# Longer times for GpSimd's operations in a scheduler's table: the same instructions of a two-layer encoder in another order

## The chip, the core and the metric

The kernel runs on one core of one Trainium2 chip. The metric is the device time of one execution in microseconds (us), the median of several runs. An engine is named as in the profile: PE is TensorE (matrix products and transposes), PEld its loading of the stationary operand, DVE is VectorE, ACT is ScalarE, POOL is GpSimd, and SP is SyncE, which here only issues DMAs.

## The reference

Two layers, each a mixer and a gated FFN, over 256 tokens of 1024 channels, in float32. Cut to what matters:

```python
def mixer_sublayer(x, n1, w_in_l, qg, kg, rpb_l, og, w_out_l, tables):
    h = rms_norm(x, n1)
    qa, ka, va, qd, kd, vd, qc, kc, vc = split(h @ w_in_l)
    out_a = neighbourhood_attention(norm(qa), norm(ka), va, rpb_l)      # 4 heads, position bias
    out_d = dilated_window_attention(rotary(norm(qd)), rotary(norm(kd)), vd)   # 6 heads, 3 window patterns
    out_c = gqa_block_attention(axial(norm(qc)), axial(norm(kc)), vc)   # 6 heads on 2 key heads
    mix = concat([rms_norm(out_a), rms_norm(out_d), rms_norm(out_c)])
    return x + mix @ w_out_l

def channel_sublayer(x, n2, w_gu, cw, cb, w_dn):
    g, u = split(rms_norm(x, n2) @ w_gu)           # 2 x 2816
    g = depthwise_conv_centred(g, cw, cb)          # 3 taps along the sequence
    return x + (gelu(g) * u) @ w_dn

for l in range(2):
    x = mixer_sublayer(x, ...)
    x = channel_sublayer(x, ...)
```

Every head has 64 channels. The norm of a head is a root mean square over these 64, so each token and head needs a power of −1/2.

## The kernel before, in words

**The numbers.** To keep float32 accuracy each operand of a large product is split into a high and a low part, and each product is three matmuls: high by high, high by low, low by high (`mm3`). ACT makes the high part of a weight (`wp_hi`) from what was loaded (`wp_raw`), DVE the low part (`wp_lo`), in chunks of 512 elements. The same is done for the activations (`act_hT`, the normed input turned; `act_mixT_hi` and `act_mixT_lo`, the heads' outputs; `act_ch` and `act_cl`, the turned probabilities).

**The mixer.** A weight comes in units of at most 2048 elements per partition, each loaded by one DMA of SP. The seven projections are, in this order, the queries, keys and values of the dilated heads ("d"), the queries and then keys with values of the grouped-query heads ("c"), and the queries with keys, then the values of the neighbourhood heads ("a"). Each goes to two accumulators in PSUM (two blocks of 128 tokens), from a pool of four slots, `psa`. `normed` then squares the accumulator (ACT), sums per head, computes the mean square (`small_ms`, one instruction on POOL) and its power of −1/2 (`small_rstd`, one on POOL, by `rstd_of`), and scales the accumulator by it (DVE, `act_z`); this reading sets the slot free for a later projection. Dilated and grouped-query heads are then rotated (DVE, `act_sw` and `act_z`, with tables that POOL makes in `tables_d` and `tables_c`), and all are turned by PE. Heads go two by two: twelve score matmuls as one burst that nothing may interrupt, a maximum (`small_nm`, or for heads with a bias an addition with minimum, `act_s2k` of the custom DVE instruction), the exponential on ACT, the reciprocal of the sum, the turning of the probabilities by PE, and the product with the values. The output of two heads is split into `act_mixT`; its square is added up (`act_sqm`, one addition on POOL per pair of heads after the first). The output projections of the three groups go to `psa` again, and DVE adds each to the residual `const_x`, scaled by the group's own power (`group_rstd`, POOL again).

**The position bias** of the neighbourhood heads is made in layer 0 on the way: POOL repeats a small table (`na_repeat`, the copy `act_nab<-act_few`), SP writes it to a scratch in DRAM and reads it back along diagonals (`na_diagonals`), and DVE adds the mask in three instructions (`na_bias_mask`).

**The FFN** has eleven steps of 256 channels. A step holds gate and up (64 matmuls), the convolution and gelu on ACT and DVE, and the product down of an earlier step (24 matmuls).

**What sets the order.** No instruction is issued where the code calls it. All of them are recorded in a `Plan` with their dependences (`add`), then `order` simulates the five engines: it repeatedly takes, over all engines, the instruction that could start soonest, and among those that tie the one of the lower rank, which is the place in the code plus a shift. An instruction's length comes from `cost`; from engine to engine a delay is added from the table `HANDOVER`; DMAs wait for the wires; buffers of a pool come in the order of the code, and an instruction that first uses a buffer waits for a slot. At the end `emit` calls them all in this order, so every instruction in the profile has line 402. The order of each engine is then fixed: on the chip an engine waits at an instruction whose inputs aren't ready, with all that is behind it.

In the model's table an instruction of POOL costs, in ns for n elements per partition: memset 40 + 0.9 n; copy 3.4 n; power 300 + 165 n; anything else 2.2 n + 160. The functions that the change and the steps touch are `cost` (line 405, the edit at 439 to 441), `order` (298, where `o.ns` is used), `rstd_of` (600), `mean_squares` (632), `tables_d` and `tables_c` (733, 748), `mixed` (1017) and `na_repeat` (715). A power has n = 6 for the dilated heads and the grouped-query queries, 2 for the grouped-query keys, 8 for the neighbourhood queries with keys, and 2 (two blocks of tokens) for a whole row or a group.

Of the kernel before, what the change touches and what calls it, by code (L numbers as in the profile page):

```python
# [216 lines left out]
class Plan:  # L217
# [30 lines left out]
    def add(self, engine, method, args, kw):  # L248
# [14 lines left out]
        if method == "matmul" and not kw["start"]:  # L263
            ins.append(args[0])
        o.ns, o.size = cost(engine.name, method, args, kw, ins)
        o.before, o.after, o.first, o.tiles = set(), [], [], []
        for v in ins + outs:
# [137 lines left out]
def cost(engine, method, args, kw, ins):  # L405

    out = args[0]
    if method == "dma_start":
        w = out if isinstance(out, View) else args[1]
        small = min(out.shape[-1], args[1].shape[-1]) < 128  # L410
        return 460, 4 * math.prod(w.shape) * (2 if small else 1)
    n = out.width()
    psum = any(v.tile.pool.psum for v in ins)
    if engine == "PE":
        if method == "transpose":
            return 110, 0
        n = args[2].width()
        if args[1].dtype == F32:
            return 108, 0
        if args[1].shape[0] < P:  # L420
            return n / 4.8 + 15, 0
        return n / (2.4 if args[1].dtype == F32R else 1.2) + 2.5, 0
    if engine == "ACT":
        extra = 93 * sum(isinstance(kw.get(k), View) for k in ("scale", "bias")) + 90 * ("accum_out" in kw)
        return 0.833 * n + (47 if psum else 94) + extra, 0
    if engine == "DVE":
        if method in ("reduce_sum", "reduce_max"):
            n = args[1].width()
        per = 1.04
        if method in ("tensor_copy", "tensor_scalar_mul") and not psum:  # L430
            per = 0.52
        if method == "tensor_tensor_reduce":
            per = 1.3
        return per * n + (130 if method == "scalar_tensor_tensor" or method == "tensor_scalar_mul" and n > 16 else 70), 0
    if method == "memset":
        return 40 + 0.9 * n, 0
    if method == "tensor_copy":
        return 3.4 * n, 0
    if kw.get("op") == ALU.pow:
        return 300 + 165 * n, 0  # L440
    return 2.2 * n + 160, 0


@with_exitstack
# [959 lines left out]
```

## Time and profile before

| | us |
|---|---|
| runs | 618.57, 619.05, 619.42 |
| median | 619.05 |
| the profiled execution | 618.73 |
| its span, from first to last instruction in the trace | 616.9 |
| PE busy | 607.5 |
| DVE busy | 487.1 |
| ACT busy | 429.8 |
| POOL busy, in 125 instructions | 78.1 |
| layer 0: second half of the FFN's first gate matmuls begins | 129.39 |
| layer 1: the same | 430.96 |

How to read it: the profiled execution lies 0.32 us under the median, and 1.83 us of it lie outside the span. In the views below a row gives the start and the length in us, the engine, the line, the operation, the output, an arrow and the inputs, the shapes and the count. In brackets stands how long the engine was idle just before and whose work ended it. A buffer is named by its pool and tag, so all accumulators of `psa` are `psa_a`, and those of the second PSUM pool, for scores, transposes, heads' outputs and gate and up, are `psw_w`. PE's matmuls are pipelined: the length of one contains its way through, so the distance from start to start tells the rate. The mixer of a layer runs about 130 us, the rest is the FFN. In both layers the FFN's first gate matmuls are in two halves, by the two halves of the channels of its normed input, which is turned by eight transposes each, and the second half needs the last output projections to be in the residual.

POOL's work is spread thinly: it is busy 3.55 us of the 20 from 60 to 80, and 5.89 of the 20 from 80 to 100. TensorE's granted clock was 1.00 in both.

### The profile page before, as it was taken

The numbers are of one execution on the slowest core, as the hardware profiler recorded it, in microseconds if no ns is written. First come the engines' busy times: TensorE is split into PE (matmuls) and PEld (weight loads), VectorE is DVE, ScalarE is ACT, GpSimd is POOL, SyncE is SP. The second block draws the span as 40 slices with busy tenths as digits, with TensorE's granted clock in tenths as the row PEclk, the third lists the DMA queues.
The fourth block names the chain that finished last, engine by engine and source line by source line (L and its number), as shares of the span: only waits on it lengthen the run. The fifth ranks groups of instructions, "written<-read, shape, count | busy, mean of one in ns | idle before, by whom it ended". The sixth has DMA issues, their size and how long they took to land.

```text
span 616.9 us, 9838 instructions
## 1 busy us (share of the span) xinstructions
PE 607.5 (98%) x3496; PEld 525.4 (85%) x3496; DVE 487.1 (79%) x1000; ACT 429.8 (70%) x1064; POOL 78.1 (13%) x125
## 2 busy tenths in 40 slices
PE   8999999999999999999999999999999999999997
PEld 6998888878888888888899989887888888888885
DVE  4898888897878777777867798979877777787775
ACT  6888898777565565556588899897756566556651
POOL 2732130111600000000023212112000000000000
PEclk9999999999999999999999999999999999999999
DMA  8894303466596566554444632127575565556501
GB/s 276 270 285 163 104 34 105 143 218 198 195 225 224 176 201 204 198 169 162 154 147 151 232 104 86 35 73 247 181 236 172 188 206 192 166 189 203 178 29 68
DMA packets 81345, 104.66 MB, mean 170 GB/s; under 512 B 9464, under 2 KB 68952, under 8 KB 81296
## 3 DMA queue, kind: packets, MB, share of 16 engines
q1 hardware_dynamic: 80720, 103.51, 52.0%
q8 instruction: 27, 0.44, 0.3%
q10 hardware_dynamic: 576, 0.53, 0.3%
q14 instruction: 22, 0.18, 0.1%
HBM read 102.54 MB, written 1.49 MB: 169 GB/s over the span
## 4 chain that ended last, share of the span: by engine, by line
PE 93%; ACT 3%; DVE 2%; DMA 1%; issue 1%; ACTq 0%
PE psw_w L402 49%; PE psa_a L402 44%; ACT act_s2k L402 2%; DMA const_x<-in_x_dram 1%; DVE wp_lo L402 1%; DVE act_hT L402 1%; ACT act_ch L402 0%; DVE const_x L402 0%; ACTq L402 0%; ACT wp_hi L402 0%; DVE small_nm L402 0%; ACT act_mixT_hi L402 0%; DVE act_z L402 0%; ACT act_sqm L402 0%; DVE small_rs L402 0%
## 5 line engine op out<-in xcount | busy, mean ns | idle before, releaser
L402 DVE TENSOR_TENSOR wp_lo<-wp_raw,wp_hi 128x512 fp32r<-128x512 f32 (+2 forms) x348 | 244.5, 732 | 48.2 <-ACT wp_hi L402 46.3
L402 PE MATMUL psw_w<-act_hT,wp_hi 128*128 128x512 f32 x704 | 247.8, 397 | 2.7 <-DVE act_hT L402 2.7
L402 ACT CAST wp_hi<-wp_raw 128x512 fp32r<-128x512 f32 (+2 forms) x348 | 213.0, 659 | 25.0 <-PE psw_w L402 15.7
L402 PE MATMUL psw_w<-act_hT,wp_lo 128*128 128x256 f32 x704 | 195.8, 279 | 0.0
L402 PEld LDWEIGHTS psw_w<-act_hT,wp_hi 128*128 128x128 f32 x704 | 131.9, 188 | 35.1 <-DVE act_hT L402 3.9
L402 PEld LDWEIGHTS psw_w<-act_hT,wp_lo 128*128 128x128 f32 x704 | 132.6, 188 | 1.1
L402 PE MATMUL psa_a<-wp_hi,act_hT 128*128 128x384 f32 (+2 forms) x448 | 113.4, 333 | 0.0
L402 ACT COPY act_s2k<-psw_w 128x256 f32<-128x256 f32 x88 | 32.4, 373 | 80.5 <-PE psw_w L402 80.5
L402 PEld LDWEIGHTS psa_a<-wp_hi,act_hT 128*128 128x128 f32 x448 | 78.7, 190 | 2.4
L402 PE MATMUL psa_a<-wp_lo,act_hT 128*128 128x384 f32 (+2 forms) x224 | 75.0, 335 | 0.0
L402 PE MATMUL psa_a<-wp_lo,act_ch 128*128 128x512 f32 x176 | 69.5, 395 | 0.0
L402 PE MATMUL psa_a<-wp_hi,act_ch 128*128 128x512 f32 x176 | 69.3, 394 | 0.0
L402 PE MATMUL psa_a<-wp_hi,act_cl 128*128 128x512 f32 x176 | 66.1, 394 | 0.0
L402 DVE TENSOR_TENSOR act_s2k<-psw_w,act_s2k 128x256 f32<-128x256 f32 x88 | 36.8, 422 | 30.6 <-ACT act_s2k L402 30.2
L402 PEld LDWEIGHTS psa_a<-wp_lo,act_hT 128*128 128x128 f32 x224 | 42.4, 189 | 2.0 <-DVE wp_lo L402 1.1
L402 PEld LDWEIGHTS psa_a<-wp_hi,act_cl 128*128 128x128 f32 x176 | 33.1, 188 | 7.8
L402 PEld LDWEIGHTS psa_a<-wp_hi,act_ch 128*128 128x128 f32 x176 | 33.1, 188 | 7.8
L402 PEld LDWEIGHTS psa_a<-wp_lo,act_ch 128*128 128x128 f32 x176 | 33.1, 188 | 6.9
L402 DVE SCALAR_TENSOR_TENSOR act_s2k<-act_s2k,act_cw,act_s2k 128x255 f32<-128x255 f32 x88 | 36.8, 478 | 1.4 <-ACT act_s2k L402 1.3
L402 ACT ACTIVATE act_s2k<-act_s2k,act_cw 128x256 f32<-128x256 f32 x44 | 24.1, 595 | 11.6 <-DVE act_s2k L402 11.6
L402 POOL TENSOR_TENSOR small_rstd<-small_ms,const_mh 128x6 f32<-128x6 f32 (+2 forms) x26 | 31.5, 1210 | 2.1
L402 ACT ACTIVATE act_s2k<-act_s2k 128x512 f32<-128x512 f32 x22 | 13.9, 632 | 22.4 <-DVE act_s2k L402 22.4
(109 smaller groups left out, 773.3 us busy)
## 6 DMA issues: line engine op xcount, KB each, us to landing
wp_raw<-in_w_gate_up_dram SPq DMA_DIRECT2D x44, 1024.0 KB, 5.0
wp_raw<-in_w_down_dram SPq DMA_DIRECT2D x22, 1024.0 KB, 4.9
wp_raw<-in_w_in_dram SPq DMA_DIRECT2D x14, 768.0 KB, 5.7
wp_raw<-in_w_in_dram SPq DMA_DIRECT2D x8, 1024.0 KB, 5.8
wp_raw<-in_w_out_dram SPq DMA_DIRECT2D x8, 768.0 KB, 4.3
wp_raw<-in_w_out_dram SPq DMA_DIRECT2D x4, 512.0 KB, 3.7
act_nab<-dram_scr SPq DMA_DIRECT2D x4, 448.0 KB, 7.1
out_dram<-const_x SPq DMA_DIRECT2D x4, 256.0 KB, 2.0
```

What stands on the lines that cost most here:

```text
L402: getattr(o.engine.real, o.method)(*map(real, o.args), **{k: real(v) for k, v in o.kw.items()})
```

## The change

The function `cost` gives longer times for three kinds of POOL's operations. A power goes from 300 + 165 n to 700 + 165 n ns; a `tensor_scalar` (the mean square, for example) gets a flat 500 in place of 2.2 n + 160; the rest (additions and multiplications of two tensors) goes from 2.2 n + 160 to 2.4 n + 300. Memset and copy keep their times.

```diff
     if method == "tensor_copy":
         return 3.4 * n, 0
+
     if kw.get("op") == ALU.pow:
-        return 300 + 165 * n, 0
-    return 2.2 * n + 160, 0
+        return 700 + 165 * n, 0
+    if method == "tensor_scalar":
+        return 500, 0
+    return 2.4 * n + 300, 0
```

No instruction is added or removed, and none gets other operands than through the slot of its buffer. Only the plan's idea of when POOL's results are there is changed, and with it the order in which `order` takes the instructions of all engines, and which slots their buffers get.

## The prediction

> **What bounds the kernel now.** I read the head of the page, the chain of work that ended last, busy time by stretch, the waits of TensorE (PE) and VectorE (DVE), and then the time lines of both engines through the two mixers.
>
> ```profile
> span 616.9 us, 9838 instructions
> PE 607.5 (98%) x3496; PEld 525.4 (85%) x3496; DVE 487.1 (79%) x1000; ACT 429.8 (70%) x1064; POOL 78.1 (13%) x125
> PE 93%; ACT 3%; DVE 2%; DMA 1%; issue 1%; ACTq 0%
> ```
>
> ```profile
> 149.34 11.29 PE psw_w L402 x64
> 160.63 5.58 PE psa_a L402 x24
> ```
>
> The second fence is from the chain. PE is busy 98% and makes 93% of the chain. GpSimd (POOL), whose prices are edited, is busy 13% and isn't named in it. One step of the FFN is 64 + 24 matmuls on PE, 11.29 + 5.58 = 16.87 us, and the next matmul starts when the last one lets it: a reordering of anything but PE's own stalls is worth nothing there. So the time is a fixed sum of PE work plus PE's stalls. The list of what PE waited for is short:
>
> ```profile
> PE psw_w L402 <- DVE act_hT L402: 2.7, 2, 1.3
> PE psa_a L402 <- DVE act_z L402: 0.5, 1, 0.5
> ```
>
> That list leaves out stalls that hide in the modelled ends of matmuls; they show as a start that comes later than the rate. On PE's time line (start, us) a matmul of 512 elements starts 0.23 after the one before, one of 256 after 0.117:
>
> ```profile
> 82.61 0.66 PE L402 MATMUL psw_w<-const_ident,act_s2k 128*128 128x128 f32 x4
> 83.73 0.50 PE L402 MATMUL psa_a<-wp_hi,act_mixT_hi 128*128 128x512 f32 x1 [0.46 <-DVE act_z L402]
> ...
> 108.85 0.40 PE L402 MATMUL psa_a<-wp_hi,act_mixT_lo 128*128 128x512 f32 x1
> 109.39 0.39 PE L402 MATMUL psw_w<-act_ch,const_v 128*128 128x256 f32 x1
> ...
> 127.03 1.03 PE L402 MATMUL psw_w<-const_ident,const_x 128*128 128x128 f32 x8
> 129.39 0.50 PE L402 MATMUL psw_w<-act_hT,wp_hi 128*128 128x512 f32 x1 [1.33 <-DVE act_hT L402]
> ```
>
> Four transposes of 0.11 after 82.61 would let the output projection start at about 83.0; it starts at 83.73 (stall 0.7). 108.85 to 109.39 holds 0.3 to 0.45 over the rate. Eight transposes from 127.03 end at about 127.9; the FFN begins at 129.39 (about 1.5). Added up in this way over both mixers, the stalls behind the start-up are some 4.0 us in layer 0 and 3.5 in layer 1. No order of the same instructions can gain more than these 7.5 us. The second limit is DVE, by stretch (span, then busy of PE, PEld, DVE, ACT, POOL):
>
> ```profile
> 60.00:80.00 20.00, 20.00 (x151) 17.62 (x151) 17.47 (x55) 17.96 (x52) 3.55 (x5) 1.00 0.26 81
> 80.00:100.00 20.00, 19.54 (x142) 16.56 (x141) 18.52 (x42) 17.86 (x51) 5.89 (x9) 1.00 0.16 52
> ```
>
> DVE has 2.53 and 1.48 us idle in these 20. What is put late there becomes late for PE.
>
> **The change part by part.** No instruction is added or taken away. The plan's prices for POOL go up, so everything behind a POOL result is planned later and other work is pulled in front of it. Laid side by side, POOL's own order is the same; 832 of PE's, 329 of DVE's and 265 of ACT's instructions have another place, all in the two mixers. Both FFN stages keep their order, so they cost nothing either way. The real lengths, against old and new price:
>
> ```profile
> L402 POOL TENSOR_TENSOR small_rstd<-small_ms,const_mh 128x6 f32<-128x6 f32 x12 | 17.2, 1434 | 0.9
> ...
> L402 POOL TENSOR_TENSOR small_rstd<-small_ms,const_mh 128x8 f32<-128x8 f32 x4 | 6.6, 1643 | 0.3
> ```
>
> The power over 6 elements took 1434 ns; the table has 300 + 6 × 165 = 1290 before and 1690 after. Over 8 it took 1643; the table has 1620 and 2020. The old prices lie nearer in both. So the plan gets no truer, only more cautious: it puts cover in front of POOL's results, and that cover delays something else.
>
> Layer 0, *queries of the dilated heads*. On DVE and POOL:
>
> ```profile
> 21.66 0.56 DVE L402 TENSOR_TENSOR act_z<-psa_a,small_rstd 128x384 f32<-128x384 f32 x1 [2.02 <-POOL small_rstd L402]
> 22.64 0.31 DVE L402 TENSOR_TENSOR act_sw<-act_z,act_sdq 128x48 f32<-128x48 f32 x2
> 24.94 1.96 DVE L402 TENSOR_TENSOR act_sw<-act_z,act_sdq 128x48 f32<-128x48 f32 x2
> ```
>
> ```profile
> 24.55 2.16 POOL L402 COPY act_nab<-act_few 28x1984 f32<-28x1984 f32 x1
> ```
>
> ```profile
> 24.56 0.51 PE L402 MATMUL psa_a<-wp_hi,act_hT 128*128 128x384 f32 x2
> 25.07 0.44 PE L402 MATMUL psa_a<-wp_lo,act_hT 128*128 128x384 f32 x1
> 25.36 0.52 PE L402 MATMUL psa_a<-wp_hi,act_hT 128*128 128x384 f32 x2
> ...
> 29.00 0.44 PE L402 MATMUL psa_a<-wp_lo,act_hT 128*128 128x384 f32 x1
> ```
>
> DVE stood 2.02 us for the power, and the low parts of weight unit 3 were queued behind it. On PE three matmuls of 384 elements lie between 24.56 and 25.36, 3 × 0.173 = 0.52 at the rate: the one at 25.07, of a low part, cost 0.28. The like around 29.00 cost 0.27. Now three of these low parts stand ahead of the scaling, in the 2.02 us: −0.55.
>
> The pair of tiny multiplications took 1.96 beside POOL's copy and 0.31 without it. The Trainium skill, page "SBUF — State Buffer", section "🎯 Summary: rules for kernel authors", says that a DVE instruction with both inputs in SBUF and a GpSimd one that reads SBUF exclude each other, the later waiting for the earlier; the two rows agree (1.96 beside the copy, 0.31 away from it). By that rule the hold of 1.65 us isn't removed by the new order but falls on whichever such instruction stands beside the copy, and the sum keeps its −0.55 only because the low parts now stand ahead of it. If a low part is the one held, −0.55 goes back to 0.
>
> Layer 0, *first output projection* (the stall of 0.7 at 83.73). PE waited there for DVE's scaling of the neighbourhood heads, which freed the accumulator, and that waited for POOL's 1.65 us power. In the new order the squares on ACT are earlier and this projection stands 0.7 us of PE work later: −0.7. Small new waits at the transposes of the grouped-query keys, about 68: +0.3, an estimate from walking the new order with the durations of these rows. The stalls from 108.85 to 114 (0.45 + 0.23 + 0.2) go, since the scores of the last two neighbourhood heads start about 0.8 us earlier: −0.9. Against it, all of the third group's output projection now stands ahead of the transposes that begin the FFN. Before, part of it stood between them and covered DVE:
>
> ```profile
> 127.01 1.13 DVE wp_lo L402 x2
> ...
> 128.90 0.45 DVE act_hT L402
> ```
>
> This is the chain: the gate opens when DVE has worked through weights and FFN input, not when PE is done, so what PE saves ahead of it is partly waited away: +0.9. Layer 0: −0.55 − 0.7 + 0.3 − 0.9 + 0.9 = −0.95.
>
> Layer 1, *scores of grouped-query heads 2 and 3*. DVE and PE before:
>
> ```profile
> 382.36 0.76 DVE L402 TENSOR_REDUCE small_nm<-psw_w 128x1 f32<-128x256 f32 x2 [0.24 <-PE psw_w L402]
> ...
> 384.61 0.68 DVE L402 TENSOR_TENSOR act_z<-psa_a,small_rstd 128x512 f32<-128x512 f32 x1
> ...
> 387.07 0.48 DVE L402 SCALAR_TENSOR_TENSOR act_mixT_lo<-psw_w,const_gains,act_mixT_hi 128x256 fp32r<-128x256 f32 x1
> ```
>
> ```profile
> 381.35 0.98 PE L402 MATMUL psw_w<-act_kc,act_qc 64*128 64x256 f32 x12
> ...
> 385.11 0.29 PE L402 MATMUL psa_a<-wp_hi,act_hT 128*128 128x256 f32 x1
> 385.34 0.50 PE L402 MATMUL psa_a<-wp_hi,act_mixT_hi 128*128 128x512 f32 x1
> ```
>
> The output projection at 385.34 takes the accumulator that the scaling at 384.61 sets free; it stalled 0.2. In the new order the twelve score matmuls stand behind 18 more projection matmuls (18 × 0.117) and three transposes (0.33), 2.4 us of PE work later. Between their end and that projection PE has only four transposes and six matmuls, 0.44 + 0.70 = 1.15 us. DVE must do in the meantime four maxima (0.76 the pair, less where they overlap: 1.4), one low part of the mix (0.48, 0.4 before the next starts) and the scaling (0.68): 2.4 to 2.6. It can begin the first maximum some 0.1 before the burst is over, so PE stands about 1.4 in place of 0.2: +1.2. Queued behind DVE's scaling are its second token block and the softmax reciprocals of heads 2 and 3.
>
> ```profile
> L402 DVE SCALAR_TENSOR_TENSOR const_x<-psa_a,small_rstd,const_x 128x512 f32<-128x512 f32 x24 | 17.5, 745 | 0.5
> ```
>
> ```profile
> 410.41 0.40 PE L402 MATMUL psa_a<-wp_hi,act_mixT_lo 128*128 128x512 f32 x1
> 410.96 0.39 PE L402 MATMUL psw_w<-act_ch,const_v 128*128 128x256 f32 x1 [0.15 <-ACT act_ch L402]
> ...
> 430.96 0.50 PE L402 MATMUL psw_w<-act_hT,wp_hi 128*128 128x512 f32 x1 [1.34 <-DVE act_hT L402]
> ```
>
> Next, head c5's transposed probabilities stand behind the neighbourhood exponentials on ACT, and their low part behind two additions to the residual on DVE (745 ns each); what PE has there covers little, and I take +0.8 and +0.6 for its two waits: bounds nothing and the two additions' whole 1.5. Gains: 0.2 at the start of the mixer, and 0.95 from 410.41 (0.55 to the next start, where 0.23 is the rate) to 416, the twins of layer 0's stalls at 108.85. FFN entry, whose gate opened at 430.96 after two stalls of 0.23 and 1.59: now 2.1, +0.3. Layer 1: +1.2 + 1.4 − 0.2 − 0.95 + 0.3 = +1.75.
>
> SyncE's queue: in layer 0 the writing and reading back of the position bias each go behind one more weight load, and two of DVE's three mask additions wait until about 59; they are needed by the first neighbourhood scores at about 100. Nothing by itself; its uncovered price is a rival below. In layer 1 the two convolution loads go ahead of one weight load: nothing, PE's weights are on hand there.
>
> Sum: −0.95 + 1.75 = +0.8. The profiled execution took 618.73 (span 616.9, 1.83 outside it), 0.32 under the median: 619.5 on its scale, **619.9** on that of the median 619.05.
>
> **Rivals.**
> *The new waits of layer 1 don't come (faster).* They rest on a walk by hand over steps of 0.1 to 0.4 us, and DVE's backlog there is what it rests on. If DVE is 1.2 ahead at the scaling and ACT 1.4 ahead at c5, both terms are gone: 619.9 − 2.6 = 617.3. In that stretch DVE was busy 4.82 of 6 us:
>
> ```profile
> 380.00:386.00 6.00, 6.00 (x53) 5.43 (x52) 4.82 (x12) 5.53 (x18) 3.52 (x4) 1.00 0.26 90
> ```
>
> For it: those 1.18 us idle. Against it: the chain scores, maxima, scaling, projection is fixed by the new order, whatever stands before.
>
> *DVE is overrun in layer 0 (slower).* The moved mask additions are these two,
>
> ```profile
> 44.44 1.43 DVE L402 SCALAR_TENSOR_TENSOR act_nab<-act_nab,const_na 128x576 f32<-128x576 f32 x2
> ...
> 57.92 0.42 DVE L402 CUSTOM_DVE_ANT_0 act_s2k<-psw_w,const_dil 128x256 f32<-128x256 f32 x1
> ```
>
> 1.43 us out of a stretch that ran partly idle into one with 2.53 idle in 20, where the biases of the dilated scores (4 × 0.42) stand as well. It decides if DVE, between the additions at 59 and the output projection at 83, can't catch up 1.43 beyond what it idles at PE's command: then the scaling in front of that projection is late by it, the 0.7 that I let go stays, and PE loses 1.43 + 0.7 = 2.1: 622.0. Against it: PE has work that doesn't need DVE in that stretch.
>
> *The low parts are held beside the copy:* 0.55 dearer, 620.45. *The order makes no difference*, since POOL's order is the same and both limits keep their sums: 619.05.
>
> **How the numbers follow.** Some 0.2%, 1.24 us, is what a measurement of this kernel tells from no change: 617.8 to 620.3. The forecast, 619.9 with ±0.8 for its two guessed terms, has 0.40, of which 0.28 lie inside the band and 0.12 above. The faster rival has 0.26; DVE overrun 0.26; the held low parts 0.04, above the band; no difference 0.04. Faster 0.26, same 0.28 + 0.04 = 0.32, slower 0.12 + 0.26 + 0.04 = 0.42. The range takes in both outer rivals and 0.8 beyond the dearer one: 617.0 to 622.8; the forecast's own is 619.1 to 620.7.
>
> **What would show it.** FFN steps still 16.87. DVE's wait of 2.02 at 21.66 gone, and no late matmul near 25 and 29. No 0.46 at the first output projection of layer 0. In layer 1 a new wait of about 1.4 of PE for DVE's scaling at about 387, and the FFN of layer 1 beginning some 0.8 later than 430.96; that of layer 0 about 0.95 before 129.39. Wrong if layer 1 shows no such wait, or if PE waits between 60 and 83.

## The result, and the profile after

The changed kernel took 619.65 us (median of 20 runs, 618.01 to 620.62), the kernel before 618.63 beside it (20 runs, 617.10 to 619.45): ratio 1.0016, 95% interval 1.0009 to 1.0023. So it is slower by some 1.0 us, a difference inside the 0.2% that the prediction took as the limit of what can be told, but clear of zero with so many runs. The profiled execution's span grew from 616.9 to 618.0.

The head of the page after, and the chain by engine:

```profile
span 618.0 us, 9856 instructions
PE 606.6 (98%) x3496; PEld 526.9 (85%) x3496; DVE 485.4 (79%) x1000; ACT 429.8 (70%) x1064; POOL 78.5 (13%) x125
PE 95%; ACT 2%; DVE 1%; DMA 1%; issue 0%; ACTq 0%
```

PE still makes the chain. All the busy sums are those of before within 0.6%; only the stalls have moved. What PE waited for, of the kernel after:

```profile
PE psw_w L402 <- DVE act_hT L402: 4.0, 4, 1.2
PE psw_w L402 <- ACT act_s2k L402: 1.3, 1, 1.3
...
PE psw_w L402 <- ACT act_ch L402: 0.4, 1, 0.4
```

The wait for `act_z` of before is gone, a new one of 1.3 for ACT's exponential (`act_s2k`) has come, and the waits for the FFN's input (`act_hT`) are four in place of two. To see all of it, stalls hidden in the modelled ends too, I added up in both traces how much later each matmul starts than the rate of the one before allows (0.232 us for 512 elements, 0.174, 0.117 and 0.110 for 384, 256 and a transpose, 0.0755 for a score on the average of a burst; a start that comes earlier counts against it). The text calls this the lateness. By stretch:

| from, to (us) | what lies there | before | after |
|---|---|---|---|
| 0, 13 | start-up, loads | 4.81 | 5.17 |
| 13, 45 | layer 0: projections of the dilated heads | 0.70 | 0.14 |
| 45, 80 | first scores, grouped-query projections | 0.98 | 1.30 |
| 80, 100 | first output projection | 1.11 | 0.73 |
| 100, 122 | last heads | 1.21 | 0.08 |
| 122, 135 | FFN entry | 1.82 | 2.97 |
| 135, 310 | FFN | 0.44 | 0.10 |
| 310, 382 | layer 1 up to head c1 | 1.37 | 1.11 |
| 382, 396 | heads c2 to c5 | 0.52 | 2.01 |
| 396, 420 | neighbourhood heads | 1.20 | 1.42 |
| 420, 435 | FFN entry | 1.92 | 2.19 |
| 435, end | FFN | 0.44 | 0.43 |

Layer 0's mixer (13 to 135) goes from 5.82 to 5.22, layer 1's (310 to 435) from 5.01 to 6.73. With start-up (+0.36) and the first FFN (−0.34) this gives +1.13, as in the spans. The last two are not the change's: PE's first 197 instructions and the whole FFN keep their order, and in the runs below the start-up was 4.1 to 6.4 and this FFN 0.10 or 0.43 with the same orders.

The place in layer 1. PE, DVE and ACT after, by time line (start, length, in brackets the idle time before):

```profile
382.93 0.98 PE L402 MATMUL psw_w<-act_kc,act_qc 64*128 64x256 f32 x12
383.83 0.66 PE L402 MATMUL psw_w<-const_ident,act_s2k 128*128 128x128 f32 x4
385.80 0.39 PE L402 MATMUL psw_w<-act_ch,const_v 128*128 128x256 f32 x1 [1.31 <-ACT act_s2k L402]
...
386.61 0.39 PE L402 MATMUL psa_a<-wp_hi,act_mixT_hi 128*128 128x512 f32 x1
```

```profile
383.94 1.42 DVE L402 TENSOR_REDUCE small_nm<-psw_w 128x1 f32<-128x256 f32 x4 [0.49 <-PE psw_w L402]
385.27 0.47 DVE L402 SCALAR_TENSOR_TENSOR act_mixT_lo<-psw_w,const_gains,act_mixT_hi 128x256 fp32r<-128x256 f32 x1
385.66 0.68 DVE L402 TENSOR_TENSOR act_z<-psa_a,small_rstd 128x512 f32<-128x512 f32 x1
```

```profile
384.73 0.47 ACT L402 ACTIVATE act_s2k<-psw_w,small_nm 128x256 f32<-128x256 f32 x1 [0.22 <-DVE small_nm L402]
...
385.19 0.47 ACT L402 ACTIVATE act_s2k<-psw_w,small_nm 128x256 f32<-128x256 f32 x1
```

The burst of scores of heads c2 and c3 runs at 382.93 (before 381.35), with nothing behind it but four transposes and the value products of c0 and c1. The first of these products at 385.80 takes the PSUM buffer in which head c2's scores lie. It is free when ACT has taken both exponentials out of it, at 385.66, and those waited for DVE's maxima. The stall is 1.47 over the rate. The output projection at 386.61 then finds its accumulator free: DVE's scaling had ended at 386.34.

### The profile page after: what moved, and what is told of

It reads as the page before. It is cut to its first block, busy times and chain, and to the rows that moved or that the text cites. A ratio compares the mean times of both kernels' runs of the same rounds, so it can differ in the third digit from the quotient of the medians.

```text
span 618.0 us, 9856 instructions
## 1 busy us (share of the span) xinstructions
PE 606.6 (98%) x3496; PEld 526.9 (85%) x3496; DVE 485.4 (79%) x1000; ACT 429.8 (70%) x1064; POOL 78.5 (13%) x125
## 3 DMA queue, kind: packets, MB, share of 16 engines
HBM read 102.54 MB, written 1.49 MB: 168 GB/s over the span
## 4 chain that ended last, share of the span: by engine, by line
PE 95%; ACT 2%; DVE 1%; DMA 1%; issue 0%; ACTq 0%
PE psw_w L402 50%; PE psa_a L402 44%; ACT act_s2k L402 1%; DMA act_s2k<-in_norm_g_dram 1%; DVE act_hT L402 0%; DVE wp_lo L402 0%; ACT act_hT L402 0%; ACT act_ch L402 0%; DVE small_nm L402 0%; DVE const_x L402 0%; DVE act_cl L402 0%; ACTq L402 0%; DVE act_mixT_lo L402 0%; ACT act_mixT_hi L402 0%; DVE act_s2k L402 0%
## 5 line engine op out<-in xcount | busy, mean ns | idle before, releaser
L402 PE MATMUL psw_w<-act_ch,const_v 128*128 128x256 f32 x128 | 29.0, 289 | 1.7 <-ACT act_s2k L402 1.3
```

The costliest lines, as they stand in the source:

```text
L402: getattr(o.engine.real, o.method)(*map(real, o.args), **{k: real(v) for k, v in o.kw.items()})
```

## The experiments

Each was timed in turn with the kernel before on the same chip; a ratio is to it.

**e1 and e2: one layer each.** A variable holds the layer that is being recorded; the old prices come back in the other layer. The orders by layer are then exactly those of the two kernels.

```diff
+    if STAGE[0] == 1:
+        if kw.get("op") == ALU.pow:
+            return 300 + 165 * n, 0
+        return 2.2 * n + 160, 0
     if kw.get("op") == ALU.pow:
         return 700 + 165 * n, 0
```

> Longer prices for the operations recorded in layer 0 only; layer 0 then has the changed kernel's order and layer 1 that of the kernel before, instruction for instruction. Theory (the two layers add up: layer 0 gains by its lost stalls, layer 1 loses by new ones): about 0.6 to 0.95 us faster than before, some 617.9 against 618.63, ratio 0.9985 to 0.999; second half of the first gate matmuls of layer 0 at about 129.1, PE's stall of 1.47 near 385.8 absent. Rival (the loss isn't from the order of the mixers but from start-up and chance): the same 1.0 us slower as the changed kernel, ratio 1.0016.

> Longer prices for layer 1 only. Theory: slower than before by the 1.7 us that the mixer of layer 1 is longer in the changed kernel's trace: 620.3 against 618.63, ratio 1.0028; the stall of 1.47 of PE ahead of the value product of heads c4 and c5's predecessors is there, and about 1.06 ahead of the scores of the last two neighbourhood heads. Rival (start-up and chance): ratio 1.0016 or 1.000, as the two layers would be alike.

Measured: layer 0 alone 618.77, ratio 0.9995 (0.9985 to 1.0006); layer 1 alone 620.35, ratio 1.0028 (1.0016 to 1.0039). The layers add up: −0.05% and +0.28% against +0.16% for both, within the intervals. Layer 1 is the whole loss. Layer 0's gain falls short of the 0.6 to 0.95 that I expected and can't be told from nothing by the time; its trace has the stalls of the changed kernel in layer 0 (13 to 135 us: 5.24). In e2's list of PE's waits stands

```profile
PE psw_w L402 <- ACT act_s2k L402: 1.3, 1, 1.3
```

and in e1's it doesn't.

**e3: four prices.** From the kernel before, only mean square and power of layer 1's grouped-query keys (n = 2, both token blocks) get the longer prices. Tiles carry their names for this.

```diff
+    name = out.tile.name
+    if not (name.split('_')[-1][:3]=='ck1'):
+        if kw.get("op") == ALU.pow:
+            return 300 + 165 * n, 0
+        return 2.2 * n + 160, 0
     if kw.get("op") == ALU.pow:
         return 700 + 165 * n, 0
```

> The kernel before, with the longer prices for four instructions only: mean square and power of the grouped-query keys of layer 1 (two elements per token block). The planned order of layer 1 then has the late burst of scores for heads c2 and c3, as in the changed kernel. Theory (this burst is what costs): slower than before by 1.4 to 1.7, 620.0 to 620.3, ratio 1.0023 to 1.0028, with a stall of about 1.4 ahead of the output of heads c0 and c1. Rival (the many small moves in layer 1 each cost a little): about 0.3 slower, ratio 1.0005.

Measured: 620.35, ratio 1.0026 (1.0015 to 1.0037), and a stall of 1.47 at 387.11 before the same value product. Four numbers out of the whole table make the late burst. The total fits less neatly than it seems: this order also stalls 0.77 a little later, saves some 0.9 at the FFN entry, and in the profiled execution lost more through the clock (last section). Nor do the four prices move the burst alone: in every trace with the late burst two waits follow between 403 and 409, some 1.1 together, and in no trace without it.

**e4: the scaling first.** In the changed kernel the scaling of the neighbourhood heads' first block goes ahead of the four maxima on DVE.

```diff
-            for i in self.order():
+            done = self.order()
+            name = lambda i, k: getattr(self.ops[i].args[k], "tile", None) and self.ops[i].args[k].tile.name
+            move = next(i for i in done if self.ops[i].engine.name == "DVE" and name(i, 0) == "z_a10")
+            done.remove(move)
+            done.insert(next(k for k, i in enumerate(done) if self.ops[i].engine.name == "DVE" and name(i, 0) == "nm_c12"), move)
+            for i in done:
```

> The changed kernel with one instruction moved: in layer 1 DVE scales the first token block of the neighbourhood heads ahead of the four maxima of heads c2 and c3, not behind them. Theory of the prediction (PE waits there for the accumulator that this scaling sets free): 1.2 to 1.4 us faster than the changed kernel, 618.3. Rival (PE waits for the PSUM buffer of the scores of head c2, which ACT's exponential sets free, and that waits for DVE's maxima): the maxima come 1.0 later since the scaling must wait for its power until 384.4, and the kernel is 0.6 to 1.0 us slower than the changed one, 620.3 to 620.7.

Measured: 621.44, ratio 1.0045 (1.0033 to 1.0057), so some 1.8 slower than the changed kernel: the rival, and more than the 0.6 to 1.0 that I gave it. PE and DVE of e4:

```profile
386.14 0.39 PE L408 MATMUL psw_w<-act_ch,const_v 128*128 128x256 f32 x1 [2.38 <-ACT act_s2k L408]
```

```profile
383.68 0.69 DVE L408 TENSOR_TENSOR act_z<-psa_a,small_rstd 128x512 f32<-128x512 f32 x1 [0.96 <-POOL small_rstd L408]
384.29 1.41 DVE L408 TENSOR_REDUCE small_nm<-psw_w 128x1 f32<-128x256 f32 x4
```

The accumulator is free at 384.4, long before PE comes to it at 386.95, and the stall is longer, not shorter: PE waits for the score buffer. In the profiled execution the stall grew by 1.07, and the clock took another 1.4 (last section).

**e5: the same four prices taken back** from the changed kernel; the test of e3's diff with `!=` in place of `==`, so that the keys alone have the old prices.

> The changed kernel with the old prices for four instructions only: mean square and power of the grouped-query keys of layer 1. The burst of scores of heads c2 and c3 is then planned where the kernel before has it. Theory (the late burst is the larger part of layer 1's loss): no stall of 1.47 ahead of the output of heads c0 and c1, and 0.9 to 1.4 us faster than the changed kernel, 618.2 to 618.8, ratio to the kernel before 0.9993 to 1.0003. Rival (the loss is spread over the many moves of layer 1): still 1.0 to 1.3 slower than before, ratio 1.0016 to 1.002.

Measured: 618.07, ratio 0.9986 (0.9977 to 0.9995). From 1.0016 to 0.9986: the four prices are worth 0.3%, 1.9 us, more than expected, and without them the change would have been a gain. The stall is gone but for 0.20 over the rate (PE of e5, 0.3 from the last projection matmul to the value product):

```profile
384.32 0.29 PE L403 MATMUL psa_a<-wp_hi,act_hT 128*128 128x256 f32 x1
384.64 0.39 PE L403 MATMUL psw_w<-act_ch,const_v 128*128 128x256 f32 x1
```

The burst is not the whole of it: from 382 to 396 the lateness falls from 2.01 to 0.64, and from 396 to 420 from 1.42 to 0.32, because the two waits that follow the burst go too. Part of the gain is given back at the FFN entry, where the lateness rises from 2.19 to 2.89:

```profile
425.37 0.50 PE L403 MATMUL psw_w<-act_hT,wp_hi 128*128 128x512 f32 x1 [1.12 <-DVE act_hT L403]
430.55 0.50 PE L403 MATMUL psw_w<-act_hT,wp_hi 128*128 128x512 f32 x1 [1.23 <-DVE act_hT L403]
```

**e6 and e7: other tables.** e6 has prices near the measured lengths, e7 only the power's line of the change.

```diff
-        return 700 + 165 * n, 0
+        return 560 + 145 * n, 0
     if method == "tensor_scalar":
-        return 500, 0
-    return 2.4 * n + 300, 0
+        return 360, 0
+    return 2.2 * n + 180, 0
```

```diff
     if kw.get("op") == ALU.pow:
         return 700 + 165 * n, 0
-    if method == "tensor_scalar":
-        return 500, 0
-    return 2.4 * n + 300, 0
+    return 2.2 * n + 160, 0
```

> Prices fitted to the durations in the trace: power 560 + 145 n (850, 1430, 1720 for 2, 6, 8 elements), tensor_scalar 360, the rest 2.2 n + 180; both layers. Theory of the prediction (the changed table loses because it is too long, so the true one should not): no late burst in layer 1, and 617.6 to 618.6, ratio 0.9985 to 1.000. Rival (how true a price is doesn't matter, any small change of it deals another order with gains and losses of some 1 us): anything from 617.4 to 620, no better than the others.

> Only the price of the power is raised (700 + 165 n); tensor_scalar and the rest stay at the old prices. The planned order of layer 1 keeps the burst of heads c2 and c3 where the kernel before has it. Theory (the loss is one place in the order, not the longer power as such): no stall of 1.47 there and within 0.6 us of the kernel before, ratio 0.9985 to 1.001. Rival (a longer power delays what needs it, wherever): 1.0 us slower than before, ratio 1.0016.

Measured: e6 618.43, ratio 0.9990 (0.9981 to 1.0000); e7 617.39, ratio 0.9974 (0.9965 to 0.9983). e7 was a miss on the good side: I had expected no change, and it gains 1.6 us. PE of e7, at the value product and at both halves of the FFN entry:

```profile
384.97 0.29 PE L402 MATMUL psa_a<-wp_hi,act_hT 128*128 128x256 f32 x1
385.29 0.39 PE L402 MATMUL psw_w<-act_ch,const_v 128*128 128x256 f32 x1
...
424.88 0.50 PE L402 MATMUL psw_w<-act_hT,wp_hi 128*128 128x512 f32 x1 [0.21 <-DVE act_hT L402]
429.83 0.50 PE L402 MATMUL psw_w<-act_hT,wp_hi 128*128 128x512 f32 x1 [1.01 <-DVE act_hT L402]
```

Its layer 1 has a lateness of 3.69, against 5.01 before and 6.73 in the changed kernel: no late burst, a first FFN wait of 0.21, and the stalls from 396 to 420 down to 0.26. Layer 0 is at 5.67, against 5.82 before.

**e8: the power and the flat 500**, the third price taken back.

```diff
     if method == "tensor_scalar":
         return 500, 0
-    return 2.4 * n + 300, 0
+    return 2.2 * n + 160, 0
```

> The changed kernel without its third price (additions and multiplications of two tensors stay at 2.2 n + 160): the power at 700 + 165 n and tensor_scalar at 500. DVE and ACT have the changed kernel's order in layer 1, PE all but 41 places. Theory (power and tensor_scalar together plan the keys' power so late that the burst of heads c2 and c3 moves): the stall of 1.4 to 1.5 is back and the kernel is 0.6 to 1.3 slower than before, ratio 1.001 to 1.002. Rival (the third price is what loses): as the run with the power alone, ratio 0.9974.

Measured: 619.58, ratio 1.0011 (1.0001 to 1.0022), with the stall of 1.47 back at 387.02. Beside e7 this lays the loss on the flat 500 for the mean square, on top of the longer power: together they put the keys' result 0.74 later in the plan than the old table for each token block, the power alone 0.40. The flat 500 without the longer power wasn't run.

**e9: the best of both**, layer 0 with the changed table and layer 1 with the power alone.

```diff
     if kw.get("op") == ALU.pow:
         return 700 + 165 * n, 0
+    if STAGE[0] == 1:
+        return 2.2 * n + 160, 0
     if method == "tensor_scalar":
```

> The changed kernel's prices in layer 0, and in layer 1 those of the run with only the power raised. The orders are those two, layer for layer. Theory (layers add up): PE's stalls from 13 to 435 us were 5.2 in layer 0 of the changed kernel and 3.7 in layer 1 of the run with the power alone, 8.9 against 10.8 before: 1.9 faster than before, 616.7 to 617.2, ratio 0.9967 to 0.9977. Rival (the layers are tied, or the rest is chance): no faster than the power alone, ratio 0.998 or more.

Measured: 617.35, ratio 0.9972 (0.9962 to 0.9982). It is faster than both kernels, but not to be told from e7, whose interval covers it: layer 0's share (a lateness of 5.23 against 5.67 in the traces) is too small for these times.

**e10: e3 again, one execution with its trace.**

> The same kernel as the run with the longer price for layer 1's grouped-query keys alone, whose times lay in two groups (619.3 to 620.4 and 621.3 to 622.2) and whose profile had TensorE's clock at 0.50 for some 3 us after two stalls. Theory (the clock is halved in some executions only, depending on when the stalls fall): either a profile without the half clock and a span some 1.3 shorter, or the same again. Rival (the stalls of 1.47 and 0.77 always halve it): the same half clock at 390 to 392.

Measured: span 618.3 against 620.4 in e3's profile, and no half clock (last section). Of these 2.1 the clock is 1.4; the rest lies in the start-up and the FFN.

## Why the prediction was right, point by point

The forecast was +0.8 us (ratio 1.0014); measured were +1.0 and 1.0016. The two layers came out near their sums as well: layer 0 −0.60 for −0.95, layer 1 +1.72 for +1.75. Part of that is luck: single terms were off by 0.2 to 0.35 and cancelled. The FFN of layer 0 began at 129.14, only 0.25 before the old 129.39 where I had 0.95, also because the start-up took 0.36 longer; that of layer 1 began at 432.09, 1.13 later where I had 0.8. And the stalls that an order could gain from were more than my 7.5: 10.8 by the count of lateness (5.82 + 5.01). By steps:

*Queries of the dilated heads, −0.55:* right, −0.56. DVE of the changed kernel:

```profile
22.29 0.55 DVE L402 TENSOR_TENSOR act_z<-psa_a,small_rstd 128x384 f32<-128x384 f32 x1
...
25.46 1.89 DVE L402 TENSOR_TENSOR wp_lo<-wp_raw,wp_hi 128x384 fp32r<-128x384 f32 x1
```

The scaling no longer waits 2.02. And the rival of the held low parts happened: a low part of 0.55 took 1.89 beside POOL's copy (25.10 to 26.94), as the rule of the Trainium skill that the prediction weighs (page "SBUF — State Buffer", section "🎯 Summary: rules for kernel authors") would have it. It cost nothing, because this part was made well ahead of its matmul; the price that I gave that rival, 0.55, was wrong.

*First output projection of layer 0, −0.7:* its stall is gone (0.117 to the start of the projection at 84.03), but other small waits came in the stretch, which is −0.38 altogether. *Keys' transposes, +0.3:* 0.26 behind them, at 69.56; with 0.21 elsewhere (62.82) and smaller ones, +0.32 from 45 to 80. *The last heads, −0.9:* −1.13. *FFN entry, +0.9:* +1.15; the two halves stalled

```profile
123.95 0.50 PE L402 MATMUL psw_w<-act_hT,wp_hi 128*128 128x512 f32 x1 [1.12 <-DVE act_hT L402]
...
129.14 0.50 PE L402 MATMUL psw_w<-act_hT,wp_hi 128*128 128x512 f32 x1 [1.23 <-DVE act_hT L402]
```

so of the 1.75 that layer 0 gained ahead (0.56 + 0.38 + 1.13 − 0.32), two thirds were waited away at the gate that DVE opens.

*The late burst of layer 1, +1.2:* +1.49, and the mechanism was right up to the last link. The step that failed is "the output projection takes the accumulator that the scaling sets free": PE never came to it. The value product ahead of it wanted the buffer of the scores, behind the same four maxima, and e4 told the two apart. The two waits end almost together, 385.66 and 386.34 with six matmuls between, so that the size came out by luck, through the wrong releaser. That both would have stalled PE I only argue: no run takes away the score buffer's wait alone.

*Head c5, +0.8 and +0.6:* too large, 0.52 and 0.54, and the second is elsewhere than I had it:

```profile
404.14 0.38 PE L402 MATMUL psw_w<-act_ch,const_v 128*128 128x256 f32 x1 [0.36 <-ACT act_ch L402]
404.45 1.39 PE L402 MATMUL psw_w<-act_ko,act_qo 64*128 64x256 f32 x12
```

The first is the wait for ACT's high part. The second falls inside the next twelve scores, which take 1.39 in place of the 0.98 of an undisturbed burst, and not at a product of c5. DVE's low part of c5, behind the two additions as I had said, ends at 404.81; it reads the PSUM buffer that goes to the second of these heads, whose first score starts at 404.86. No run tests this wait by itself.

*Gains from 410 on, −0.95, FFN entry +0.3:* with c5's two terms the stretch from 396 to 420 is +0.22, where the prediction has +0.45; the entry is +0.27. *Overrun of DVE in layer 0:* not seen, no single stall of PE over 0.3 between 60 and 83.

The reason that I gave for the loss was wrong, though. The prediction said that a table further from the measured times makes the plan only more cautious, and that its cover in front of POOL's results delays something else. The power alone is as far off (1690 for 1434 ns) and gives the fastest table tried but for its own mixture. The step looked at the power by itself, where POOL's mean square, a gap and the power come one after the other: for the keys the old prices sum to 0.794 us, the new ones to 1.53, the power alone to 1.19; before the change they took 1.06 in layer 1 (0.27, a gap of 0.09 and 0.70). Nor do true prices decide: e6 gained 0.1%, e7 0.26%. Ten tables dealt orders between 617.35 and 620.35 us, and in the traces of layer 1 they differ in a few places: the late burst with the two waits that follow it, and the FFN entry (1.04 to 2.89).

## What to carry to other kernels

When a scheduler's table is edited, don't ask whether the price is truer; lay the two orders side by side and look, in front of every wait, for the work that covered it. A burst moved later on the bounding engine costs its followers' cover, not its own time, and the same buffers come free in a row there, so removing one wait may only uncover the next (argued here from e4, not shown by a run that removes one). Test prices one by one and by stage: here the prices of four instructions of two elements turned a gain of 0.14% into a loss of 0.16%.

## What the runs showed of the hardware that I had not expected

After a stall TensorE can run at half clock for some 3.4 us, and whether it does varies from execution to execution with the same stalls. Windows of e4 (span, busy time of PE, PEld, DVE, ACT and POOL, granted clock):

```profile
384.00:386.20 2.20, 0.06 (x1) 0.06 (x1) 2.16 (x7) 1.13 (x5) 2.12 (x3) 1.00 0.00 0
386.20:388.00 1.80, 1.80 (x9) 1.61 (x10) 1.68 (x5) 1.80 (x7) 0.23 (x1) 0.71 0.00 0
388.00:390.00 2.00, 2.00 (x7) 1.62 (x7) 1.19 (x3) 1.13 (x4) 0.00 (x0) 0.50 0.00 0
390.00:392.00 2.00, 2.00 (x12) 1.69 (x12) 1.15 (x3) 1.58 (x5) 0.00 (x0) 0.91 0.00 0
```

PE resumes at 386.14 at full rate and falls to half at 386.95, until about 390.3: matmuls of 512 elements start 0.43 apart in place of 0.23. The stretch from 382 to 396 has 4.44 of lateness, of which the stall is 2.54. In e3 the two stalls of 1.47 and 0.77, 2.2 apart, were followed by it; the same window in e3 and then in e10, the same kernel:

```profile
390.00:392.40 2.40, 2.40 (x8) 1.92 (x8) 2.40 (x7) 1.87 (x6) 0.00 (x0) 0.50 0.00 0
```

```profile
390.00:392.40 2.40, 2.40 (x18) 2.18 (x17) 2.40 (x8) 2.40 (x9) 0.00 (x0) 1.00 0.00 0
```

Eight matmuls against eighteen, a lateness of 4.04 against 2.63 from 382 to 396: 1.4 us by the clock. The eleven times of e3 lie in two groups, 619.27 to 620.39 and 621.29 to 622.24, but the half clock alone doesn't make the second: one stretch of 3.4 us at half takes 0.003 off an execution's mean granted clock, and of the four slow executions only two show that (0.997 and 0.994), the other two have 1.000, and one of the faster seven has 0.997. What made those two slow is open. All five executions of e4 have 0.996 or 0.997, of the changed kernel's twenty five.

Why the same stalls trip it in one execution and not in another can be worked out from the traces. In each of them the granted clock changes only at whole multiples of 3.41 us after full clock was first granted, and that first moment differs by execution (4.67 in e4, 9.60 in e10, 10.40 in e3). Cut into these stretches, PE was idle (its ends as the profile models them) for 2.38 of the 3.41 us just ahead of e4's half clock (383.55 to 386.96) and for 1.86 ahead of e3's (385.86 to 389.27). In e10 a boundary, at 388.48, fell between the same two stalls: 1.38 idle in one stretch, 0.54 in the next, and the clock stayed. In all the traces half clock followed every stretch with 1.86 or more, counted from there on, and none with 1.44 or less; with 1.79 it followed once and once not (both in e6).

The Trainium skill, page "TensorE: Matmul & The Clock Gate", section "🎯 Why this matters for your kernels", advises against gaps above about 3 us between bursts of matmuls. Here one gap of 2.38 did it, and once two of 1.31 and 0.61; the measurement decides. In the changed kernel's profile, with the one gap of 1.31, the clock stayed at 1.00. So stalls of 2 us that fall into one such stretch may cost 1.4 more than they show, and in a study of tenths of a per cent this is the size of the effects themselves.
